# Four scheduling edits in a hybrid S5 and retention decoder layer: priority of the first evacuations and of the last chunk's scan, spacing of the chunks, issuing engine of sixteen copies

## The chip, the cores and the metric

The kernel runs on one core of a Trainium2 chip. The metric is the device time of one execution in microseconds (us); lower is better. The engines are named as in the profile: PE multiplies matrices, DVE works on vectors, ACT evaluates functions and copies, POOL does small vector work, SP issues transfers. A transfer can also be issued from ACT's instruction stream. Each engine takes its instructions in the order of its own queue.

## The reference, cut to what matters

One inference step of one decoder layer on 320 columns: 256 prompt positions, and 64 sample columns (8 sequences of 8 positions). All data are float32.

```python
proj = h @ w_in                                   # u, q, k, v, g
s5_out, s5_re, s5_im = s5_mixer(u, ...)           # diagonal state scan, 64 groups of 16 channels
o, ret_new = retention_chunked(q, k, v, ret0)     # 8 heads, decayed attention and state
o = (o - mu) * lax.rsqrt(var + NORM_EPS)          # per-head norm
ret_out = silu(g) * o * ret_gn_w
x = x + concat([s5_out, ret_out]) @ w_out
gate, up = split(rms_norm(x) @ w_ffn_in)
x = x + (silu(gate) * up) @ w_ffn_out
```

The S5 state follows `x[t] = lam_bar * x[t-1] + b_bar u[t]` and gives `y = Re(C x) + D u`, then a GELU and a gated unit. The retention states of the 8 sample sequences are updated too: `r_new = r * decay + k^T v`.

## The kernel before, in words

**Products.** Every weight block is split into two parts, `hi` (rounded) and `lo` (the rest), and a product is three PE passes: hi by hi, hi by lo, lo by hi. `wload` (line 121) loads half a weight block of 128 x 1024 values (`raw`), has ACT cast it to `hi` (line 130) and DVE subtract to get `lo` (line 131). Three buffers of `hi` and of `lo` are there, so a block's half can be prepared when an older half has been used up. `gemm` (line 135) issues the passes, 48 matmuls for 16 steps of k, into one of two PSUM accumulators (tag `acc`).

**Order of the work.** The orders of PE and POOL are written by hand. PE's is set by a model clock: a step of k (three matmuls) adds 0.4, and `run_due` after a step lets every waiting generator run whose due time has come, so its matmuls are put between two steps. The delays are in `DL` (line 807). The orders of DVE, ACT and SP are found by a list scheduler, which takes ready instructions by priority: the place in the program, moved ahead by the `offset` of `tc.high_priority`. `wload` has 3000, most evacuations of accumulators have `EVAC` = 1500.

**First stage** (lines 825 to 871). Four products run side by side into four accumulators: u of chunk 0 (`ps0`, the tile `py0`), u of chunk 1 (`ps1`, first half of `pb0`), q of head 0 (`pq`, second half of `pb0`), k of head 0 (`pk`, an `acc` accumulator). `finish_norm` (line 860) waits for the norm's factor `rbc`, multiplies the rotation tables `csr` by it with `EVAC` priority, and multiplies `ps0` and `ps1` into `u32` at lines 869 and 870 with none. At the same time DVE works through `s5_params` (line 363), a long chain of small operations on `tab` and `ecs`; from `ecs` POOL makes the tables of `s5_tables` (line 462), and only then, in POOL's written order, the norm of head 0 (`gy`, lines 704 to 711). ACT makes `on` from `gy` (line 714), PE transposes `on` into `pn` (line 725).

**Chunks.** `s5_chunk` (line 502) treats 8 groups of channels at a time, 8 chunks in all. It prepares its operators on DVE (`bl`, `cl`), has PE transpose them (`pt`), multiplies into `pb` (line 554), scans the states on DVE (lines 574 to 601: `t`, `ends`, `w`, the scan, `v`, then `xp`), and multiplies `xp` into `py` (lines 603 to 613). Chunk c starts when the model clock is at `T0 + PER * c`, `pt` comes 14.2 later, `pb` 6.6 after that, `py` 17.8 after that. After the last projection (`do_g(7)`), lines 912 and 913 run the model clock forward until the last chunk's `py` has been issued.

**After the projections.** `split_r` (line 945) splits the heads' outputs into `r4a` and `r4b` for the product with `w_out`; `r4a` lies in the memory of `tab`, which the last chunk's `v` still reads. `x1` is loaded from `xT` (line 907), into memory that the projections have read.

**Sample states.** During the first gate of the FFN `states_split` (line 1036), with an offset of 6000, splits `kv` into `kvh` and `kvl` in the weight buffers and spreads them with 16 copies from SBUF to SBUF (lines 1050 and 1051), 128 KB each, issued by SP. They write into `hi` and `lo` buffers that the first gate (`ps_fg`) has just read. `states_load` and `states_add` use them later.

Of the kernel before, what the change touches and what calls it, by code (L numbers as in the profile page):

```python
# [12 lines left out]
F32 = mybir.dt.float32  # L13
# [4 lines left out]
ADD, SUB, MUL = ALU.add, ALU.subtract, ALU.mult  # L18
PSUM = bass.MemoryType.PSUM

P = 128
# [12 lines left out]
NCP = NP // CH  # L34
NC = N // CH
# [9 lines left out]
def hybrid_kernel(ctx, tc, xT, w_in, w_in4, w_out, w_glu, w_fi, w_fo, vecs, s5p, bc, x0,  # L45
# [3 lines left out]
    pe, act, dve, pool, sp = nc.tensor, nc.scalar, nc.vector, nc.gpsimd, nc.sync  # L49
# [5 lines left out]
    def f(t):  # L55
        return t.bitcast(F32)
# [44 lines left out]
    def mm(cost, *a, **k):  # L101
        pe.matmul(*a, **k)
        clk.now += cost
# [71 lines left out]
    def tt(out, a, b, op):  # L175
        dve.tensor_tensor(out, a, b, op)  # L176
        return out
# [11 lines left out]
            stt(y, tmp, 1.5, y, ADD, MUL)  # L189

    STARTS = (0, 128, 192)

    def rstd_bcast(pool_, acc, ps_of, tag, last=None, dl=5.0, ytok=None):

        def sums(a, name):
            ps = ps_of(name)
            for i, s in enumerate(STARTS):
                mm(0.1, ps[:, i:i + 1], a[:, s:s + P], ones[:, 0:1], start=True, stop=True)
            return ps[:, 0:3]

        ms = pool_.tile([P, 3], F32, name="ms", tag=tag + "ms")
        y = pool_.tile([P, 3], F32, name="ry", tag=tag + "ry")
        if ytok is not None:
            ytok.append(y)
        tmp = pool_.tile([P, 3], F32, name="rt", tag=tag + "rt")
        ps = sums(acc, "ps_r")
        if last is not None:
            keep_warm(3)
        with tc.high_priority(offset=2000):
            ts(ms, ps, -0.5 / D, MUL, -0.5 * EPS, ADD)  # L210
            if last is not None:
                stt(ms, sums(last(), "ps_l"), -0.5 / D, ms, MUL, ADD)
            if last is not None:
                keep_warm(9)
            rsqrt(ms, y, tmp)
        yield dl
        ps2 = ps_of("ps_r2")
        for i, s in enumerate(STARTS):
            mm(0.22, ps2[:, s:s + P], y[:, i:i + 1].to_broadcast([P, P]), ident, start=True,
               stop=True)  # L220
        yield ps2[:, :N]
# [12 lines left out]
    s5 = s5stack.enter_context(tc.tile_pool(name="s5", bufs=1, side="right"))  # L234
# [9 lines left out]
    rbc = mp.tile([P, N], F32, name="rbc")  # L244
# [13 lines left out]
    u32 = up.tile([P, 8, N], F32, name="u32")  # L258
# [37 lines left out]
    x0t = s5.tile([P, 2, NPAIR, NB], F32, name="x0t")  # L296
    tab = s5.tile([P, 2, NPAIR, NCP], F32, name="tab", tag="tab", bufs=1)
# [10 lines left out]
    lx0 = s5.tile([P, 2, NPAIR, NB], F32, name="lx0")  # L308
    endp = s5.tile([P, 2, NPAIR], F32, name="endp")
    ends = s5.tile([P, 2, 2, NPAIR, NB], F32, name="ends")  # L310
# [186 lines left out]
    def load_bc(c):  # L497
        if c < 8:
            raws[c] = s5.tile([P, 2, 8, 16], F32, name="raw_bc", tag="raw_bc", bufs=3)
            sp.dma_start(raws[c], bc[:, c])  # L500

    def s5_chunk(c):
        load_bc(c + 2)
        js = slice(4 * c, 4 * c + 4)
        cl, xp, d0 = cls_[c % 2], xps[c % 2], d0s[c % 2]
# [19 lines left out]
        for w_, pc in ((0, gpc), (1, lpc)):  # L525
# [4 lines left out]
            if w_ == 0:  # L530

                bl = s5.tile([P, 2, 2, 2, CH, 16], F32, name="bl", tag="bl", bufs=1)
                for r, (a, b, op) in enumerate(((m1[:, 0:4], m2[:, 4:8], SUB), (m1[:, 4:8], m2[:, 0:4], ADD))):
                    a, b = (t_.rearrange("p (u q) e h -> p u q (e h)", q=2) for t_ in (a, b))
# [19 lines left out]
        pb = ps_b.tile([P, 2, 512], F32, name="pb", tag="pb", bufs=1)  # L554
        for i in range(4):
            for u in range(2):

                for g in range(2):
                    us, gs = slice(64 * u, 64 * u + 64), slice(64 * g, 64 * g + 64)
# [9 lines left out]
        for u in range(2):  # L569
            for g in range(2):  # L570
                hs = slice(16 * g, 16 * g + 16)
                act.copy(kbd[64 * g:64 * g + 64, 2 * u:2 * u + 2, hs],
                         pk_[64 * u:64 * u + 64, 0:64].rearrange("p (i h) -> p i h", h=32)[:, :, hs])
        pvs = [pb[:, u, 0:4 * NC].rearrange("p (r q t) -> p r q t", r=2, q=2) for u in range(2)]
        shr = [P, 2, 4, NCP]
        tb = [tab[:, q, js].unsqueeze(1).to_broadcast(shr) for q in range(2)]
        t = [s5.tile(shr, F32, name=f"t{q}", tag=f"m{q}", bufs=1) for q in range(2)]
        w = s5.tile(shr, F32, name="w", tag="w", bufs=1)
        for q in range(2):
            for u in range(2):  # L580
                us = slice(2 * u, 2 * u + 2)
                tt(t[q][:, :, us], pvs[u][:, :, :, 0:NCP], tb[q][:, :, us], MUL)
        for u in range(2):
            us = slice(4 * c + 2 * u, 4 * c + 2 * u + 2)
            psm = pvs[u][:, :, :, NCP:].rearrange("p r q (b s) -> p r q b s", s=2)
            tt(ends[:, 0, :, us], psm[:, :, :, :, 0], lx0[:, :, us], ADD)
            act.copy(ends[:, 1, :, us], psm[:, :, :, :, 1])
        tt(w[:, 0], t[0][:, 0], t[1][:, 1], ADD)
        tt(w[:, 1], t[0][:, 1], t[1][:, 0], SUB)
        wf = w.rearrange("p r j t -> p (r j t)")  # L590
        dve.tensor_tensor_scan(wf, d0.rearrange("p r j t -> p (r j t)"), wf, 0.0, MUL, ADD)
        act.copy(endp[:, :, js], w[:, :, :, NCP - 1])
        t = [s5.tile(shr, F32, name=f"v{q}", tag=f"m{q}", bufs=1) for q in range(2)]
        for q in range(2):
            tt(t[q], w, tb[q], MUL)
        tt(xp[:, 0, :, 1:NCP], t[0][:, 0, :, 0:NCP - 1], t[1][:, 1, :, 0:NCP - 1], SUB)
        tt(xp[:, 1, :, 1:NCP], t[0][:, 1, :, 0:NCP - 1], t[1][:, 0, :, 0:NCP - 1], ADD)
        xs = xp[:, :, :, NCP:].rearrange("p r j (b q) -> p r j b q", q=2)
        for r in range(2):
            act.copy(xs[:, r, :, :, 0], x0t[:, r, js])  # L600
            act.copy(xs[:, r, :, :, 1], ends[:, 0, r, js])
        yield DL["scan"]
        py = ps_y.tile([P, 512], F32, name="py", tag="y", bufs=1)
        for j in range(4):
            r = 32 * j
            mm(0.15, py[r:r + 32, 0:N], kbd[:, j], ush[:, j].rearrange("p s c -> p (s c)"), start=True,
               stop=False, tile_position=(0, r))
        for t in range(CH):
            for q in range(2):
                for j in range(4):  # L610
                    r = 32 * j
# [14 lines left out]

    EVAC = 1500
    GN = 1000  # L630
    GAM = [1.0 - 2.0 ** (-5.0 - h) for h in range(H)]
    rot_t = {}

    def rot(ps, name):
        assert rot_t["ready"]
        with tc.high_priority(offset=EVAC):
            return rot_(ps, name)
# [11 lines left out]
    def head_k(h, q_, qg, k_, R):  # L649
        yield DL["k"]  # L650
        pst = misc("pst")
        for i, s in enumerate(STARTS):
            tr(pst[:, P * i:P * i + P], k_[:, s:s + P])
# [9 lines left out]
        mk = R["mk"]  # L663
        with tc.high_priority(offset=EVAC):
            tt(sm[:, 0:256], pss[:, 0:256], mk[:, 0:NP], MUL)
# [5 lines left out]
    def head_v(h, v_, qg, rt, R):  # L671
        yield DL["v"] + (3.0 if h == 0 else 0.0)
        pst2 = misc("pst2")
        for i, s in enumerate(STARTS):
            tr(pst2[:, P * i:P * i + P], v_[:, s:s + P])
# [21 lines left out]
        y = mp.tile([P, 2, 4], F32, name="gy", tag="gy", bufs=1)  # L697
        with tc.high_priority(offset=GN):
            for i in range(4):
# [42 lines left out]
    def proj(i):  # L742
        return gemm("ps_p", w_in[i], KT, xhi, xlo)
# [7 lines left out]
    def do_u(c):  # L751
        ps = proj(c)
        with tc.high_priority(offset=EVAC):
            tt(u32[:, c], ps, rbc, MUL)
# [24 lines left out]
    def do_v(h, ps=None):  # L779
        ps = proj(10 + 4 * h) if ps is None else ps  # L780
        R = HS[h]
        v_ = mp.tile([P, N], F32, name="v_", tag="v_", bufs=1)
        with tc.high_priority(offset=EVAC):
            act.copy(v_, ps)
# [3 lines left out]
    def sg_mul(h, sg):  # L788
        while "gn" not in HS[h]:
            yield 1.0  # L790
        if "sg" in HS[h]:
            return
        with tc.high_priority(offset=EVAC):
            tt(retp[:, h], retp[:, h], sg, MUL)
        HS[h]["sg"] = True

    def do_g(h):
        ps = proj(11 + 4 * h)
        sg = mp.tile([P, N], F32, name="sg", tag="sg", bufs=2)
        with tc.high_priority(offset=EVAC):  # L800
            tt(sg, ps, rbc, MUL)
# [4 lines left out]

    DL = dict(b1=14.2, b2=6.6, scan=17.8, k=8.5, v=6.1,
              o=2.2, u=6.0, c=10.0, n2=2.4, n2b=2.6, nm=0.8)
    T0, PER = 54.6, 34.0


    clk.now = 8.0
# [12 lines left out]
    for k1 in (1, *range(2, KT + 1, 2)):  # L825
        with tc.high_priority(offset=100000), tc.manual_schedule(engines={mybir.EngineType.SP}):
# [3 lines left out]
            q = slice(k0 % 2, (k1 - 1) % 2 + 1)  # L830
# [19 lines left out]
    ps0, ps1, pq, pk = accs  # L850
# [9 lines left out]
    def finish_norm():  # L860
        next(rg)
        act.copy(rtok, ytok[0])
        yield 4.5
        rps = next(rg)
        with tc.high_priority(offset=EVAC):
            act.copy(rbc, rps)
            tt(csr[:, 0], csr[:, 0], rbc, MUL)
            tt(csr[:, 1], csr[:, 1], rbc, MUL)
        tt(u32[:, 0], ps0, rbc, MUL)
        tt(u32[:, 1], ps1, rbc, MUL)  # L870
        rot_t["ready"] = True

    spawn(finish_norm(), DL["nm"])
# [30 lines left out]
    xp = ctx.enter_context(tc.tile_pool(name="xp", bufs=1, reuse_waits="tile"))  # L904
# [96 lines left out]
    for n in range(KT):  # L1001
# [8 lines left out]
        else:  # L1010
            s = square(n, hp)
# [22 lines left out]
    SU = {}  # L1034

    def states_split():

        with tc.high_priority(offset=6000):
            states_split_()

    def states_split_():
        kvh, kvl = (wp.tile([P, 8, P], F32R, name=n, tag=n, bufs=3) for n in ("hi", "lo"))
        act.copy(kvh, kv)
        tt(kvl, kv, f(kvh), SUB)
        SU["k"] = [wp.tile([P, 8, P], F32R, name="hi", tag="hi", bufs=3) for _ in range(2)]
        SU["v"] = [wp.tile([P, 8, P], F32R, name="lo", tag="lo", bufs=3) for _ in range(2)]
        for i in range(2):
            for a in range(4):
                d = slice(32 * a, 32 * a + 32)
                sp.dma_start(f(SU["k"][i][d]), f((kvh, kvl)[a // 2][64 + 32 * i:96 + 32 * i]))  # L1050
                sp.dma_start(f(SU["v"][i][d]), f((kvh, kvl)[a % 2][32 * i:32 * i + 32]))

    def states_load(h):
        rt = wp.tile([P, NB, P], F32, name="raw", tag="raw", bufs=3)
# [181 lines left out]
```

## Time and profile before

| | |
|---|---|
| median of 3 runs (lowest to highest) | 1475.02 us (1472.91 to 1475.27) |
| the profiled execution | 1475.36 us, of it 1473.6 us span |
| busy in the span: PE, DVE, ACT, POOL | 98%, 58%, 41%, 7% |
| granted PE clock, mean | 0.993 |

The profile records every instruction of one execution. Times are counted from the first instruction. Idle time before an instruction stands in brackets with the engine that ended it. A PE that is busy by the profile need not run at full clock; the granted clock is listed for each stretch. The span is divided among the projections and the mixers (to 368 us), the output product and the gated unit (to 520 us), the FFN, and a tail.

### The profile page before, as it was taken

To read this page: it belongs to the slowest core of one execution; us is meant where nothing else is said; L and a number is where in the kernel's file an instruction comes from. 1 tells how busy PE (TensorE), PEld (TensorE's weight loads), DVE (VectorE), ACT (ScalarE), POOL (GpSimd) and SP (SyncE) were. 2 spreads that over 40 slices of the span, in tenths; PEclk is the share of its full clock that TensorE was granted. 3 is DMA by queue.
4 is the path that set the end of the run, shared out by engine and by line. 5 is a ranking of instruction groups with operands and counts; after the bars stand their busy time and mean duration, and the time that the engine had idled before them with its cause. 6 is when DMAs were issued, how large, how long until landed. Compare 5 with 4: busy or idle time off the path is not lost.

```text
span 1473.6 us, 26372 instructions
## 1 busy us (share of the span) xinstructions
PE 1444.0 (98%) x10654; PEld 1426.7 (97%) x10654; DVE 854.3 (58%) x1405; ACT 607.6 (41%) x973; POOL 101.8 (7%) x228
## 2 busy tenths in 40 slices
PE   8999999999899999999999999999999999999997
PEld 8899999999899999999999999999999999999996
DVE  8887776777656765565444444444444445444454
ACT  6455555554335543333333333333333333333352
POOL 1324404210000000000000000000000000000001
PEclk9999999999999999999999999999999999999999
DMA  8555554544544474665444455444445544445443
GB/s 260 167 152 159 159 164 155 156 151 133 188 148 147 154 243 162 223 212 175 148 153 146 123 154 171 151 154 147 134 144 153 171 150 151 146 123 156 151 145 111
DMA packets 84713, 235.39 MB, mean 160 GB/s; under 512 B 16368, under 2 KB 32368, under 8 KB 84592
## 3 DMA queue, kind: packets, MB, share of 16 engines
q1 hardware_dynamic: 84448, 233.68, 49.8%
q8 instruction: 84, 1.38, 0.4%
q14 instruction: 37, 0.30, 0.1%
q10 hardware_dynamic: 144, 0.04, 0.0%
HBM read 222.63 MB, written 8.95 MB: 157 GB/s over the span
## 4 chain that ended last, share of the span: by engine, by line
PE 69%; DVE 1%; issue 0%; ACT 0%; DVEq 0%
PE ps_fo L143 7%; PE ps_fo L142 7%; PE ps_fu L143 7%; PE ps_fu L142 7%; PE ps_fu L141 7%; PE ps_fo L141 7%; PE ps_fg L143 7%; PE ps_fg L141 7%; PE ps_fg L142 7%; PE ps_o L142 1%; PE ps_o L141 1%; PE ps_o L143 1%; PE ps_g L142 1%; PE ps_g L143 1%; PE ps_g L141 1%; DVE x L176 0%
## 5 line engine op out<-in xcount | busy, mean ns | idle before, releaser
L131 DVE TENSOR_TENSOR lo<-raw,hi 128x1024 fp32r<-128x1024 f32 (+1 forms) x416 | 468.1, 1126 | 392.1 <-ACT hi L130 391.2
L130 ACT CAST hi<-raw 128x1024 fp32r<-128x1024 f32 (+1 forms) x416 | 402.0, 967 | 680.1 <-PE ps_fo L142 189.3
L141 PE MATMUL ps_fg<-hhi,hi 128*128 128x320 f32 x704 | 217.7, 309 | 1.1 <-ACT hi L130 1.1
L143 PE MATMUL ps_fg<-hhi,lo 128*128 128x320 f32 x704 | 217.6, 309 | 0.7 <-DVE lo L131 0.7
L141 PE MATMUL ps_fo<-ahi,hi 128*128 128x320 f32 x704 | 217.6, 309 | 0.0
L142 PE MATMUL ps_fo<-alo,hi 128*128 128x320 f32 x704 | 217.6, 309 | 0.0
L143 PE MATMUL ps_fo<-ahi,lo 128*128 128x320 f32 x704 | 217.6, 309 | 0.0
L142 PE MATMUL ps_fu<-hlo,hi 128*128 128x320 f32 x704 | 217.5, 309 | 0.0
L142 PE MATMUL ps_fg<-hlo,hi 128*128 128x320 f32 x704 | 217.5, 309 | 0.0
L141 PE MATMUL ps_fu<-hhi,hi 128*128 128x320 f32 x704 | 217.4, 309 | 0.0
L143 PE MATMUL ps_fu<-hhi,lo 128*128 128x320 f32 x704 | 217.4, 309 | 0.0
L141 PE MATMUL ps_p<-xhi,hi 128*128 128x320 f32 x560 | 178.4, 318 | 5.2 <-DVE sg L176 3.2
L143 PE MATMUL ps_p<-xhi,lo 128*128 128x320 f32 x560 | 173.9, 311 | 0.7 <-DVE lo L131 0.7
L142 PE MATMUL ps_p<-xlo,hi 128*128 128x320 f32 x560 | 173.6, 310 | 0.0
L141 PEld LDWEIGHTS ps_fg<-hhi,hi 128*128 128x128 f32 x704 | 132.4, 188 | 1.6 <-ACT hi L130 1.3
L143 PEld LDWEIGHTS ps_fg<-hhi,lo 128*128 128x128 f32 x704 | 132.4, 188 | 1.0 <-DVE lo L131 1.0
L142 PEld LDWEIGHTS ps_fg<-hlo,hi 128*128 128x128 f32 x704 | 132.4, 188 | 0.3
L142 PEld LDWEIGHTS ps_fu<-hlo,hi 128*128 128x128 f32 x704 | 132.4, 188 | 0.0
L141 PEld LDWEIGHTS ps_fu<-hhi,hi 128*128 128x128 f32 x704 | 132.4, 188 | 0.0
L143 PEld LDWEIGHTS ps_fu<-hhi,lo 128*128 128x128 f32 x704 | 132.4, 188 | 0.0
L141 PEld LDWEIGHTS ps_fo<-ahi,hi 128*128 128x128 f32 x704 | 132.2, 188 | 0.0
L142 PEld LDWEIGHTS ps_fo<-alo,hi 128*128 128x128 f32 x704 | 132.2, 188 | 0.0
(402 smaller groups left out, 1977.9 us busy)
## 6 DMA issues: line engine op xcount, KB each, us to landing
raw<-w_fi SPq DMA_DIRECT2D x176, 512.0 KB, 3.7
raw<-w_in SPq DMA_DIRECT2D x79, 512.0 KB, 4.0
raw<-w_fo SPq DMA_DIRECT2D x64, 512.0 KB, 3.5
raw<-w_out SPq DMA_DIRECT2D x32, 512.0 KB, 3.7
raw<-w_fo SPq DMA_DIRECT2D x64, 192.0 KB, 2.4
rt<-r SPq DMA_DIRECT2D x8, 512.0 KB, 5.0
raw<-w_glu SPq DMA_DIRECT2D x8, 512.0 KB, 3.6
raw<-r SPq DMA_DIRECT2D x8, 512.0 KB, 4.0
```

What stands on the lines that cost most here:

```text
L130: act.copy(hi[:, :m], raw[:, :m])
L131: dve.tensor_tensor(lo[:, :m], raw[:, :m], f(hi[:, :m]), SUB)
L141: pe.matmul(ps, hi, xhi[:, k], start=k == 0, stop=False)
L142: pe.matmul(ps, hi, xlo[:, k], start=False, stop=False)
L143: pe.matmul(ps, lo, xhi[:, k], start=False, stop=k == nk - 1)
```

## The change

Lines 574 to 601 become a function `s5_scan`, word for word, called with a priority offset for chunk 7 alone (0 for the others). `EVAC` and `GN` are only defined earlier. The two evacuations in `finish_norm` move into the block with `EVAC` priority. `T0` and `PER` become smaller. `states_split` loses its priority, and its 16 copies are issued by ACT.

```diff
+    EVAC = 1500
+    GN = 1000
...
+    def s5_scan(c, pb, xp, d0):
+        js = slice(4 * c, 4 * c + 4)
         pvs = [pb[:, u, 0:4 * NC].rearrange("p (r q t) -> p r q t", r=2, q=2) for u in range(2)]
...
+        with tc.high_priority(offset=2 * EVAC if c == 7 else 0):
+            s5_scan(c, pb, xp, d0)
         yield DL["scan"]
...
-    T0, PER = 54.6, 34.0
+    T0, PER = 53.6, 33.4
...
-        tt(u32[:, 0], ps0, rbc, MUL)
-        tt(u32[:, 1], ps1, rbc, MUL)
+            tt(u32[:, 0], ps0, rbc, MUL)
+            tt(u32[:, 1], ps1, rbc, MUL)
...
     def states_split():
-
-        with tc.high_priority(offset=6000):
-            states_split_()
-
-    def states_split_():
         kvh, kvl = (wp.tile([P, 8, P], F32R, name=n, tag=n, bufs=3) for n in ("hi", "lo"))
...
-                sp.dma_start(f(SU["k"][i][d]), f((kvh, kvl)[a // 2][64 + 32 * i:96 + 32 * i]))
-                sp.dma_start(f(SU["v"][i][d]), f((kvh, kvl)[a % 2][32 * i:32 * i + 32]))
+                act.dma_start(f(SU["k"][i][d]), f((kvh, kvl)[a // 2][64 + 32 * i:96 + 32 * i]))
+                act.dma_start(f(SU["v"][i][d]), f((kvh, kvl)[a % 2][32 * i:32 * i + 32]))
```

## Rows read from the trace of the kernel before

**Rows 1.** The page: busy time; the costliest groups (busy us, mean ns).

```profile
PE 1444.0 (98%) x10654; PEld 1426.7 (97%) x10654; DVE 854.3 (58%) x1405; ACT 607.6 (41%) x973; POOL 101.8 (7%) x228
...
L131 DVE TENSOR_TENSOR lo<-raw,hi 128x1024 fp32r<-128x1024 f32 (+1 forms) x416 | 468.1, 1126 | 392.1 <-ACT hi L130 391.2
```

**Rows 2.** PE's waits in the whole span: us in total, times, longest us.

```profile
PE py L102 <- DVE xp L176: 6.2, 1, 6.2
PE ps_p L141 <- DVE sg L176: 3.2, 1, 3.2
...
PE ps_p L141 <- DVE k__3502 L176: 1.3, 1, 1.3
...
PE ps_fg L141 <- ACT hi L130: 1.1, 1, 1.1
PE ps_fg L143 <- DVE lo L131: 0.7, 1, 0.7
```

**Rows 3.** PE's timeline, last chunk (first row: chunk 6): start, us, instruction.

```profile
344.43 1.29 PE L102 MATMUL py<-xp,cl 128*32 128x80 f32 x64
...
368.27 0.74 PE L102 MATMUL py<-ush,kbd 128*32 128x320 f32 x8
375.25 2.43 PE L102 MATMUL py<-xp,cl 128*32 128x80 f32 x64 [6.23 <-DVE xp L176]
...
380.94 0.31 PE L159 MATMUL ps_o<-r4a,hi 128*128 128x320 f32 x1
```

**Rows 4.** Stretches: us, busy PE (x), PEld, DVE, ACT, POOL, granted clock, DMA.

```profile
58.00:60.00 2.00, 2.00 (x9) 2.00 (x8) 2.00 (x11) 0.00 (x0) 0.47 (x1) 0.50 0.93 290
...
376.00:378.00 2.00, 2.00 (x53) 1.78 (x45) 1.21 (x6) 0.00 (x0) 0.00 (x0) 0.50 1.00 384
...
1000.00:1100.00 100.00, 100.00 (x684) 100.00 (x684) 47.62 (x61) 34.69 (x44) 0.00 (x0) 1.00 0.45 142
```

**Rows 5.** DVE's timeline, last chunk, from its first to its last product.

```profile
359.90 0.76 DVE L176 TENSOR_TENSOR t<-pb,tab 128x256 f32<-128x256 f32 x2 [1.60 <-PE pb L102]
...
373.48 1.29 DVE L176 TENSOR_TENSOR r4b<-retp,r4b 128x320 fp32r<-128x320 f32 x3
374.69 0.74 DVE L176 TENSOR_TENSOR xp<-v,v 128x252 f32<-128x252 f32 x2
```

**Rows 6.** The tile x: from 365 to 390 us, landing of its four loads.

```profile
DMA to landing us min/median/max: 5.9/7.4/10.1
```

**Rows 7.** PE's and ACT's timelines at the first evacuations.

```profile
56.71 0.60 PE L141 MATMUL ps_p<-xhi,hi 128*128 128x320 f32 x1 [3.23 <-DVE sg L176]
...
53.26 0.42 ACT L641 COPY sw<-pb 64x320 f32<-64x320 f32 x1 [2.31 <-DVE u L176]
```

**Rows 8.** Timelines of POOL, ACT and PE: from the tables to the head's norm.

```profile
59.53 0.57 POOL L474 COPY tab<-ecs 128x8 f32<-128x8 f32 x1 [51.73 <-DVE ecs L176]
...
73.65 0.24 POOL L704 TENSOR_SCALAR mv<-mv 128x4 f32<-128x4 f32 x1
...
78.21 1.50 ACT L714 ACTIVATE on<-po,gy 128x128 f32<-128x128 f32 x4 [3.92 <-POOL gy L711]
...
78.86 1.24 PE L107 MATMUL pn<-ident,on 128*128 128x128 f32 x4
```

**Rows 9.** Timelines of SP, ACT and PE at the copies of the sample states.

```profile
525.22 0.60 SPq L1050 DMA_DIRECT2D hi<-hi  x1
...
535.38 48.67 SPq L129 DMA_DIRECT2D raw<-w_fi  x18
...
525.31 1.05 ACT L130 CAST hi<-raw 128x1024 fp32r<-128x1024 f32 x1 [2.81 <-DMA raw<-w_fi]
...
529.65 0.31 PE L141 MATMUL ps_fu<-hhi,hi 128*128 128x320 f32 x1
```

**Rows 10.** DMA issues: queue, count, KB each, median us to landing.

```profile
hi<-hi SPq DMA_DIRECT2D x4, 128.0 KB, 2.9
```

**Rows 11.** The tile kst: issues on SP, ns min/median/max, first and last start.

```profile
L515 SPq DMA_DIRECT2D kst<-via x64: 325/424/1349, 56.8 to 336.3; - x64
```

More of the change, by code (lines that the diff above doesn't have):

```diff
@@ L500, in load_bc @@
             sp.dma_start(raws[c], bc[:, c])
+    def s5_scan(c, pb, xp, d0):
+        js = slice(4 * c, 4 * c + 4)
+        pvs = [pb[:, u, 0:4 * NC].rearrange("p (r q t) -> p r q t", r=2, q=2) for u in range(2)]
+        shr = [P, 2, 4, NCP]
+        tb = [tab[:, q, js].unsqueeze(1).to_broadcast(shr) for q in range(2)]
+        t = [s5.tile(shr, F32, name=f"t{q}", tag=f"m{q}", bufs=1) for q in range(2)]
+        w = s5.tile(shr, F32, name="w", tag="w", bufs=1)
+        for q in range(2):
+            for u in range(2):
+                us = slice(2 * u, 2 * u + 2)
+                tt(t[q][:, :, us], pvs[u][:, :, :, 0:NCP], tb[q][:, :, us], MUL)
+        for u in range(2):
+            us = slice(4 * c + 2 * u, 4 * c + 2 * u + 2)
+            psm = pvs[u][:, :, :, NCP:].rearrange("p r q (b s) -> p r q b s", s=2)
+            tt(ends[:, 0, :, us], psm[:, :, :, :, 0], lx0[:, :, us], ADD)
+            act.copy(ends[:, 1, :, us], psm[:, :, :, :, 1])
+        tt(w[:, 0], t[0][:, 0], t[1][:, 1], ADD)
+        tt(w[:, 1], t[0][:, 1], t[1][:, 0], SUB)
+        wf = w.rearrange("p r j t -> p (r j t)")
+        dve.tensor_tensor_scan(wf, d0.rearrange("p r j t -> p (r j t)"), wf, 0.0, MUL, ADD)
+        act.copy(endp[:, :, js], w[:, :, :, NCP - 1])
+        t = [s5.tile(shr, F32, name=f"v{q}", tag=f"m{q}", bufs=1) for q in range(2)]
+        for q in range(2):
+            tt(t[q], w, tb[q], MUL)
+        tt(xp[:, 0, :, 1:NCP], t[0][:, 0, :, 0:NCP - 1], t[1][:, 1, :, 0:NCP - 1], SUB)
+        tt(xp[:, 1, :, 1:NCP], t[0][:, 1, :, 0:NCP - 1], t[1][:, 0, :, 0:NCP - 1], ADD)
+        xs = xp[:, :, :, NCP:].rearrange("p r j (b q) -> p r j b q", q=2)
+        for r in range(2):
+            act.copy(xs[:, r, :, :, 0], x0t[:, r, js])
+            act.copy(xs[:, r, :, :, 1], ends[:, 0, r, js])
     def s5_chunk(c):
@@ L573, in s5_chunk @@
                          pk_[64 * u:64 * u + 64, 0:64].rearrange("p (i h) -> p i h", h=32)[:, :, hs])
[L574 to L601, printed above, removed]
+        with tc.high_priority(offset=2 * EVAC if c == 7 else 0):
+            s5_scan(c, pb, xp, d0)
         yield DL["scan"]
@@ L624, in s5_chunk @@
             s5_state["done"] = True
-    EVAC = 1500
-    GN = 1000
     GAM = [1.0 - 2.0 ** (-5.0 - h) for h in range(H)]
```

## The prediction

> **What bounds the kernel now.** The page comes first: PE is busy 98% of the span [rows 1], and the change takes no matmul away. It can only win PE's idle time and the time that PE runs at half clock. The list of PE's waits says who ends that idle time [rows 2]; five of its entries lie near the edits: 6.2 us for `xp` of the last chunk, 3.2 us for an evacuation (`sg`) after the norm, 1.3 us for `k` of head 4, and 1.1 and 0.7 us for `hi` and `lo` of an FFN weight. Together 12.5 us, 0.8% of the time. The stretches then show what a long wait costs behind it: the granted clock is 0.50, the 1.2 GHz level, from 58 to 60 us and from 376 to 378 us, after the two longest of these waits, and 1.00 in the steady FFN, where a matmul takes 100 us / 684 = 0.146 us [rows 4]. The timelines around each wait, last, tell whether its time is free to be won.
>
> **The last chunk: 8.9 us.** PE's first part of `py` starts at 368.27, then PE waits 6.23 us for `xp` [rows 3]. From 375.25 to 380.94 it does the second part and twelve `w_out` matmuls: 5.69 us, where chunk 6's second part took 1.29 us [rows 3] and twelve matmuls at full clock take 12 x 0.146 = 1.75 us. So 2.65 us went to the half clock, and the stall costs 6.23 + 2.65 = 8.9 us.
>
> Two edits act on it, and either nearly suffices. The start of chunk 7 moves by 1.0 + 7 x 0.6 = 5.2 of the model clock; a step of 0.4 there is three matmuls, 0.44 us, so `pb` comes 5.2 / 0.4 x 0.44 = 5.7 us earlier, while `py` stays behind the last projection, which it already followed at once. DVE's chain ran from 359.90 to 375.43 [rows 5]; begun 5.7 us earlier it ends at 369.7, against 375.25 - 6.23 = 369.0, when PE asks. The priority then takes out of the chain what doesn't belong to it: the three `r4b` splits right ahead of `xp` alone are 1.29 us [rows 5]. I take the wait as gone, and the clock with it. The price is that the chain may hold up a weight's `lo` on DVE; each is 1.13 us [rows 1] and is prepared half a gemm, 24 x 0.146 = 3.5 us, or more before its use, so I cost it at 0, at most one `lo`, 1.1 us.
>
> What is late next? `r4b` of the last head was split at 374.8 [rows 5]; PE would ask for it after `py` (369.0 + 1.29), 24 matmuls of `r4a` and nine of `r4b` (4.8 us), at 375.1. Without the chain in the way DVE and ACT have it sooner. The loads of `x1` are issued from 368.4 and take 5.9 to 10.1 us [rows 6]: the first lands between 374.3 and 378.5, and the third output block needs its accumulator free after 48 matmuls, at 377.3. Between 0 and 1.2 us; I take 0, as the first issued is nearest to the shortest landing.
>
> **The first evacuations: 0.** The wait before 56.71 is for `sg`, behind the two multiplications into `u32` on DVE and, through them, ACT's copies `sw` (idle 2.31 us until `u`) [rows 7]. With priority the two go right after the tables `csr`, and q, `sg` and k follow sooner: 3.2 us of wait, and with some 1.5 us of half clock (between 0 and the 2.65 of the last chunk) 4.7 us. But that is the whole at 57 us. At 78.86 PE transposes `on` of head 0, and it came there only 0.3 us after ACT's first of four pieces (1.50 / 4 each): ACT had idled 3.92 us for POOL, POOL reached that norm at 73.65 after tables begun at 59.53, and these had waited for `ecs` [rows 8]. The change moves the two multiplications within the DVE work that already lay ahead of that `ecs`; it takes nothing out. So `on` comes no sooner, PE stands at `pn` 4.7 us early, and the gain is given back there. Bounds: +4.7 us if `on` also comes sooner, and a loss of two `lo`, 2.3 us, if a faster PE pulls DVE's prioritised work ahead of `ecs`. I take 0, the value of the chain as it stands.
>
> **The spacing of the other chunks: 0.** Chunk c comes 1.1 to 5.1 us sooner, and DVE's bursts meet other heads. Before, one of them cost a wait, 1.3 us for `k` [rows 2]. It may go, stay, or have a twin: +1.3 to -1.3 us.
>
> **The sample states' copies: 1.8 us.** SP issues 16 copies from 525.22; the next weight load of the FFN leaves at 535.38 [rows 9], and its `hi` and `lo` are the waits of 1.1 and 0.7 us. Each copy takes 10.16 / 16 = 0.635 us of SP. On ACT they leave SP free, so the loads go out some ten us earlier and this wait goes: 1.8 us. The 10.2 us now stand in ACT's queue, behind them its casts, one per 3.5 us at 1.05 us each; spread out they fit, and the lost offset lets casts (3000) go first. What costs is a block. The first eight can start when the gate's first half is read, at about 525.2; at 525.31 ACT casts the up product's first weight, which PE uses at 529.65 [rows 9]. Eight copies ahead of it (5.1 us) move its `lo` to 525.3 + 5.1 + 1.05 + 1.13 = 532.6, a stall of 2.9 us. Bounds: +1.8 to -2.9 us and, as after 3.2 us, up to 1.5 us of clock. I take +1.8, as the cast carries the higher priority.
>
> The row of a copy's landing, 2.9 us against 0.635 us of issue [rows 10, 9], bears on a rule. The Trainium skill, "DMA: Bandwidth & Descriptors", section "Issuing engines are not separate DMA queues", says that issuing from several engines saves only the sequencer's time, usually small beside the transfer. By it this part would give about 0. The row speaks against "small" here: the issue times of sixteen add up in front of a load.
>
> **Sum.** The profiled execution took 1475.36 us (span 1473.6 and 1.8 around it), 0.34 above the median. 1475.36 - 8.9 - 0 - 0 - 1.8 = 1464.7; against the median of 1475.02 that is **1464.3 us**.
>
> **Rivals.**
> - *The first evacuations' gain is kept.* For: 4.7 us are really lost there. Against: rows 8. 1464.3 - 4.7 = 1459.6 us.
> - *ACT's copies come in a block of eight ahead of the cast.* For: at 525.2 both become ready within 0.1 us. Against: priority. 1464.3 + 1.8 + 2.9 = 1469.0 us, with the clock 1470.5.
> - *Moving the issue saves nothing*, because the loads are then held by the transfers. For: 16 x 128 KB of copies still move at the same time. Against: the load left only after the last copy [rows 9]. 1464.3 + 1.8 = 1466.1 us. The Trainium skill's rule above would make this of it.
> - *The last chunk does not profit*, its wait taken over by another of equal length (`r4b`, `x1`). For: `r4b` was ready 0.3 us before the time at which it is then wanted. Against: its delay came from the chain itself. 1475.0 - 1.8 = 1473.2 us, within 0.2%.
> - *Slower:* all sixteen copies stand on ACT ahead of the first cast. At p us each the stall is 525.3 + 16p + 2.2 - 529.65 = 16p - 2.15, plus 2.65 of half clock. It outweighs the 8.9 + 1.8 from p = 0.64 on, just SP's own pace, and at the longest issue that a small copy took, 1.35 us [rows 11], it is 22.1 us: 1486.4 us. Against: the second eight wait for the gate's second half, and casts go first.
>
> **How the numbers follow.** My forecast 0.56, evacuations kept 0.13, block of eight 0.15, issue saves nothing 0.07, last chunk without profit 0.05, slower 0.04. The range of 1459.5 to 1470.0 takes in the first four but for the block with its clock, and the bounds of chunks and `lo`. A measurement of this kernel can tell about 0.2%, 3 us. Faster by more: 0.91; within: 0.05; slower: 0.04.
>
> **What would show it.** Right: no wait of PE for `xp`, full clock from 366 to 385 us, no wait in the second FFN gate, and a new wait of 3 to 5 us at `pn` near 75 to 79 us while the one before 56.7 is short. Wrong: `pn` without a wait and everything after it 4 us sooner; PE waiting for `hi` of the first `ps_fu` with copies ahead of it on ACT; or a wait for `r4b` or an accumulator after `py`.

## The result and the profile after

The kernel after takes 1464.2 us (median of 4 runs, 1463.93 to 1465.08), the one before 1474.97 us (median of 4, 1472.91 to 1475.27). The ratio is 0.9931, with a 95% interval from 0.9914 to 0.9948: 10.8 us less. The profiled execution of after took 1463.95 us, 1461.8 us of it span, against 1475.36 and 1473.6 us. The forecast was 1464.3 us.

The page answers to [rows 1]. PE has the same 10654 matmuls, and it is busy for 4.2 us less (1439.8 against 1444.0): the same matmuls took less time. Of this, 3.4 us lie ahead of the FFN, where fewer matmuls ran at half clock. The queue line q10 had 144 packets before; the copies' 768 packets moved there from q1.

```profile
PE 1439.8 (98%) x10654; PEld 1423.1 (97%) x10654; DVE 853.1 (58%) x1405; ACT 607.6 (42%) x973; POOL 101.7 (7%) x228
...
q10 hardware_dynamic: 912, 2.14, 0.5%
```

PE's waits of after, as in [rows 2] (us in total, times, longest):

```profile
PE pn L107 <- ACT on L720: 2.3, 1, 2.3
...
PE ps_p L141 <- DVE k__3551 L176: 1.1, 1, 1.1
...
PE ps_p L141 <- DVE k__794 L176: 0.5, 1, 0.5
```

Gone are `xp` (6.2), `sg` (3.2), the two of `ps_fg` (1.1 and 0.7) and `k__3502` (1.3). New are `on` at `pn` (2.3), `k__3551` (1.1) and `k__794` (0.5). All five waits that the prediction named (12.5 us) are gone, and 3.9 us came back in other places.

**The last chunk.** PE's timeline, as in [rows 3] (start, us, instruction):

```profile
367.49 0.75 PE L102 MATMUL py<-ush,kbd 128*32 128x320 f32 x8
368.06 1.29 PE L102 MATMUL py<-xp,cl 128*32 128x80 f32 x64
...
371.14 0.31 PE L159 MATMUL ps_o<-r4a,hi 128*128 128x320 f32 x1
```

The second part of `py` follows the first without a bracket, so without a wait, and takes 1.29 us as in a chunk at full clock. The last row shown is the matmul that stood at 380.94 before: 9.80 us earlier. At `py` the lead was 368.27 - 367.49 = 0.78 us, so the last chunk itself gave 9.0 us. The stretches, as in [rows 4] (us, busy PE, PEld, DVE, ACT, POOL, granted clock, DMA), have the clock at 1.00, its 2.4 GHz level, at 58 us as well:

```profile
58.00:60.00 2.00, 1.73 (x13) 1.68 (x13) 1.94 (x13) 1.36 (x5) 1.02 (x6) 1.00 0.75 249
...
368.00:370.00 2.00, 2.00 (x73) 1.82 (x66) 1.70 (x4) 2.00 (x5) 0.00 (x0) 1.00 0.86 257
...
376.00:378.00 2.00, 2.00 (x15) 2.00 (x15) 2.00 (x4) 1.05 (x1) 0.00 (x0) 1.00 1.00 415
```

DVE's timeline, as in [rows 5], shows the chain begin at 354.04, 5.9 us earlier than before, and end at 361.0, 7 us before PE asks. `r4b` now comes behind it and still in time:

```profile
354.04 1.41 DVE L176 TENSOR_TENSOR t<-pb,tab 128x256 f32<-128x256 f32 x4
...
360.25 0.75 DVE L176 TENSOR_TENSOR xp<-v,v 128x252 f32<-128x252 f32 x2
...
370.52 1.29 DVE L176 TENSOR_TENSOR r4b<-retp,r4b 128x320 fp32r<-128x320 f32 x3
```

**The first evacuations.** Timelines of PE, POOL, ACT and PE again, as in [rows 7, 8]:

```profile
54.00 0.41 PE L141 MATMUL ps_p<-xhi,hi 128*128 128x320 f32 x1 [0.53 <-DVE k__794 L176]
...
58.32 0.55 PE L107 MATMUL pst<-ident,v__798 128*128 128x128 f32 x3 [0.27 <-ACT kv L663]
...
58.82 0.20 POOL L477 COPY tab<-ecs 128x8 f32<-128x8 f32 x1 [51.01 <-DVE ecs L176]
...
73.40 0.24 POOL L710 TENSOR_SCALAR mv<-mv 128x4 f32<-128x4 f32 x1
...
76.65 1.51 ACT L720 ACTIVATE on<-po,gy 128x128 f32<-128x128 f32 x4 [8.12 <-POOL gy L717]
...
77.16 1.38 PE L107 MATMUL pn<-ident,on 128*128 128x128 f32 x4 [2.31 <-ACT on L720]
```

In before the second of these rows is

```profile
62.51 0.55 PE L107 MATMUL pst<-ident,v__798 128*128 128x128 f32 x3 [0.27 <-ACT kv L657]
```

so PE leads by 2.7 us at the third projection (54.00 against 56.71) and by 4.2 us at head 0's `v`, where the half clock no longer stands in between; 1.2 us of both leads are the earlier start of `csr` (47.37 against 48.55, below). At `pn` it waits for 2.31 us and keeps a lead of 1.7 (77.16 against 78.86). POOL still works through the tables from 58.82 before it reaches head 0's norm at 73.40, 0.25 us earlier than before.

**The copies.** Timelines of SP, ACT's queue, ACT and PE, as in [rows 9]:

```profile
510.04 11.00 SPq L129 DMA_DIRECT2D raw<-w_fi  x7
...
515.45 0.61 ACTq L1051 DMA_DIRECT2D hi<-hi  x1
...
533.70 1.05 ACT L130 CAST hi<-raw 128x1024 fp32r<-128x1024 f32 x1 [2.47 <-DMA hi<-lo]
533.72 0.52 ACTq L1052 DMA_DIRECT2D lo<-lo  x1
...
551.27 0.51 ACTq L1052 DMA_DIRECT2D lo<-lo  x1
```

SP issues weight loads only. The 16 copies lie between ACT's casts from 515.45 to 551.27, one or two to a cast.

**A ruler for all runs.** Between executions the first stage starts at different times, because one early transfer comes sooner or later (last section). So each profile is cut at three marks: DVE's first product into `csr`, the first weight load of the FFN's gate (`ps_fg`), and that of its output product (`ps_fo`). The rows of before, then of after:

```profile
48.55 0.88 DVE L176 TENSOR_TENSOR csr<-csr,rbc 128x320 f32<-128x320 f32 x2
...
L141 PEld LDWEIGHTS ps_fg<-hhi,hi x704: 186/188/192, 520.4 to 1295.4; 128*128 128x128 f32 x176
...
L141 PEld LDWEIGHTS ps_fo<-ahi,hi x704: 187/188/189, 838.2 to 1457.3; 128*128 128x128 f32 x176
```

```profile
47.37 0.89 DVE L176 TENSOR_TENSOR csr<-csr,rbc 128x320 f32<-128x320 f32 x2
...
L141 PEld LDWEIGHTS ps_fg<-hhi,hi x704: 187/188/192, 510.6 to 1282.9; 128*128 128x128 f32 x176
...
L141 PEld LDWEIGHTS ps_fo<-ahi,hi x704: 187/188/189, 825.8 to 1444.9; 128*128 128x128 f32 x176
```

For before that is 520.4 - 48.55 = 471.9, 838.2 - 520.4 = 317.8, and 1473.6 - 838.2 = 635.4 us. The same three rows give the table for all kernels (us; the first four numbers add up to the span):

| kernel | `csr` at | to `ps_fg` | to `ps_fo` | to the end | median |
|---|---|---|---|---|---|
| before | 48.55 | 471.9 | 317.8 | 635.4 | 1474.97 |
| after | 47.37 | 463.2 | 315.2 | 636.0 | 1464.20 |
| e1_evac | 47.32 | 471.9 | 318.1 | 635.4 | 1474.43 |
| e2_scan | 47.83 | 465.0 | 318.0 | 635.3 | 1467.27 |
| e3_space | 47.61 | 462.8 | 319.5 | 635.4 | 1464.90 |
| e4_copies | 46.98 | 471.2 | 315.2 | 636.0 | 1470.67 |
| e5_no_scan_prio | 46.91 | 463.3 | 315.1 | 636.0 | 1463.46 |
| e6_tables_late | 47.64 | 460.4 | 315.2 | 636.0 | 1460.83 |
| e7_act_prio | 46.27 | 463.3 | 328.1 | 636.3 | 1476.40 |
| e8_sp_no_prio | 47.70 | 463.3 | 320.0 | 635.4 | 1468.20 |
| e9_tables_only | 47.68 | 460.6 | 315.2 | 636.0 | 1460.79 |
| e10_no_evac | 47.03 | 462.9 | 315.1 | 636.1 | 1463.23 |
| e11_after_again | 46.51 | 463.3 | 315.1 | 636.1 | 1463.74 |
| e12_tables_again | 46.19 | 460.4 | 315.1 | 636.0 | 1459.19 |

For two profiles of one kernel the ruler repeats to 0.1 us (after, e11; e6, e12), where medians of the same kernel differ by up to 1.6 us. It is not always that fine: before and e4, whose code is the same up to `ps_fg`, differ by 0.7 us there, and e2 and e3, whose code is the same from there on, by 1.5 us in the next column, where e3 alone fell to half clock. For after against before it says: 1.2 us by chance of the start, 8.7 us between `csr` and the FFN, 2.6 us in the FFN's first part, and 0.6 us lost at the end. With the rounding that is 11.8 us, the difference of the spans. A further 0.3 us is lost outside the span: the executed time is 2.1 us longer than the span in after and 1.8 us in before.

### The profile page after: what moved, and what is told of

Read it like the earlier page. It is cut to its first block, busy times and chain, and to the rows that moved or that the text cites. A ratio compares the mean times of both kernels' runs of the same rounds, so it can differ in the third digit from the quotient of the medians.

```text
span 1461.8 us, 26364 instructions
## 1 busy us (share of the span) xinstructions
PE 1439.8 (98%) x10654; PEld 1423.1 (97%) x10654; DVE 853.1 (58%) x1405; ACT 607.6 (42%) x973; POOL 101.7 (7%) x228
## 4 chain that ended last, share of the span: by engine, by line
PE 70%; DVE 0%; issue 0%; ACT 0%; DVEq 0%
PE ps_fg L141 7%; PE ps_fo L143 7%; PE ps_fo L142 7%; PE ps_fu L143 7%; PE ps_fg L143 7%; PE ps_fu L142 7%; PE ps_fg L142 7%; PE ps_fu L141 7%; PE ps_fo L141 7%; PE ps_o L143 1%; PE ps_o L141 1%; PE ps_o L142 1%; PE ps_g L142 1%; PE ps_g L143 1%; PE ps_g L141 1%; DVE x L176 0%
```

## The experiments

They were run in three groups, each beside its own runs of before (medians 1474.38, 1474.02 and 1474.49 us). The first four kernels are before with one of the four edits.

**e1_evac: before, with the two multiplications into `u32` under `EVAC` priority.**

```diff
-        tt(u32[:, 0], ps0, rbc, MUL)
-        tt(u32[:, 1], ps1, rbc, MUL)
+            tt(u32[:, 0], ps0, rbc, MUL)
+            tt(u32[:, 1], ps1, rbc, MUL)
```

> The kernel before with one edit: the two multiplications into u32 get EVAC priority. My theory (the gain is given back at pn, because POOL makes the tables ahead of head 0's norm): PE's wait before the third projection falls from 3.2 to about 0.5 us and its half clock goes, PE then waits 2 to 3 us for on at pn, and what is left at 85 us is 1.5 us, the amount by which on comes sooner in the changed kernel; 1473.5 us. Rival, the gain is kept: no wait at pn, 1470.3 us. Rival, it is lost wholly or turns into a loss: 1475 us or more.

Measured: 1474.43 us, ratio 1.0004 [0.9995, 1.0013]. The wait for `sg` is gone, and its time stands at `pn`:

```profile
PE pn L107 <- ACT on L714: 2.3, 1, 2.3
```

The ruler gives 471.9 us, that of before to the tenth. The edit alone is worth nothing, where I had expected 1.5 us; the rival that expected 1470.3 us falls.

**e2_scan: before, with `s5_scan` and its priority for chunk 7.**

```diff
+        with tc.high_priority(offset=2 * EVAC if c == 7 else 0):
+            s5_scan(c, pb, xp, d0)
```

> The kernel before with one edit: the last chunk's scan gets priority 3000, the spacing stays. My theory (either edit alone nearly suffices): the chain still starts at 359.9 and now takes some 7 us, as in the changed kernel, so xp is there by 367, ahead of the 369 at which PE asks; no wait, no half clock, 8.9 us less: 1466.1 us. Rival, the earlier start is what counts: xp after 370, a wait of 1 us or more stays, 1467 to 1471 us.

Measured: 1467.27 us, ratio 0.9953 [0.9941, 0.9966]. The wait for `xp` is gone, but another stands behind it. DVE's and PE's timelines of e2:

```profile
366.70 0.74 DVE L176 TENSOR_TENSOR xp<-v,v 128x252 f32<-128x252 f32 x2
...
370.90 0.88 DVE L176 TENSOR_TENSOR r4a<-retp,r4a 128x320 fp32r<-128x320 f32 x2
...
371.84 0.41 PE L160 MATMUL ps_o<-r4a,hi 128*128 128x320 f32 x1 [1.64 <-DVE r4a L176]
```

The priority shortens the chain from 15.5 us to 8.3 (359.19 to 367.4), but `r4a` follows it, in the memory of `tab` that the chain's `v` reads, and PE asks for it right after `py`. The ruler gives 465.0 us: 6.9 of the 8.7 us. By the medians it is 7.1 us less than before, where 8.9 were expected.

**e3_space: before, with the chunks closer together.**

```diff
-    T0, PER = 54.6, 34.0
+    T0, PER = 53.6, 33.4
```

> The kernel before with one edit: T0 and PER as in the changed kernel. My theory: the last chain begins 5.7 us sooner and still takes some 15 us, so xp comes at about 369.7, a wait of about 0.7 us without half clock; 8.2 us less, minus up to 0.8 us that the closer chunks cost between 85 and 367 us: 1466.8 to 1467.6 us. Rival, the priority is what counts: a wait of 3 us or more stays, 1470 us or more.

Measured: 1464.9 us, ratio 0.9939 [0.9927, 0.9952]: better than either number expected. DVE's and PE's timelines of e3, without any priority on the scan:

```profile
353.81 1.08 DVE L176 TENSOR_TENSOR t<-pb,tab 128x256 f32<-128x256 f32 x3
...
361.47 0.41 DVE L176 TENSOR_TENSOR xp<-v,v 128x252 f32<-128x252 f32 x1
...
367.85 1.29 PE L102 MATMUL py<-xp,cl 128*32 128x80 f32 x64
```

Begun 6.1 us earlier, the chain takes 8.1 us instead of 15.5 by itself: DVE's rows between its first `t` and `xp` hold one `lo` in e3, in before three and all splits of `r4a` and `r4b`, which in e3 come behind `xp`. The ruler gives 462.8 us, all of the gain. Its FFN, where SP still issues the copies, has the old waits of 1.2 and 0.7 us, and this time half clock behind them (stretches of e3; 319.5 us on the ruler):

```profile
534.00:536.00 2.00, 2.00 (x9) 2.00 (x8) 1.25 (x2) 0.21 (x1) 0.00 (x0) 0.50 0.74 248
```

**e4_copies: before, with the copies on ACT and without the offset.**

```diff
-        with tc.high_priority(offset=6000):
-            states_split_()
...
-                sp.dma_start(...)
+                act.dma_start(...)
```

> The kernel before with one edit: states_split without priority, its copies issued by ACT. My theory: the waits of 1.1 and 0.7 us in the second FFN gate go, nothing comes in their place, 1.8 to 2.0 us less: 1473.0 us. Rival (only the issue time moves, the loads are held by the transfers): the waits stay, 1475.0 us. Rival (copies stand ahead of casts on ACT): a wait of 2.9 us at the first up product, 1476 us or more.

Measured: 1470.67 us, ratio 0.9976 [0.9967, 0.9985]. Both waits of `ps_fg` are gone, and that stretch is 317.8 - 315.2 = 2.6 us shorter. The end is 0.6 us longer, as in every kernel whose copies ACT issues, and 0.3 us more is lost outside the span (2.1 against 1.8 us in all eleven runs): 1.7 us net. The medians differ by more, 3.7 us (2.2 to 4.9 by the interval), where 1.8 to 2.0 us were expected. In e4's profile 0.7 us more are won ahead of the FFN, where it runs the same code as before; what the medians show beyond the 1.7 us is not explained by the edit.

**e5_no_scan_prio: after, without the scan's priority.**

```diff
-        with tc.high_priority(offset=2 * EVAC if c == 7 else 0):
+        with tc.high_priority(offset=0):
```

> The changed kernel without the priority of the last chunk's scan. My theory (the earlier start alone nearly suffices): the chain takes some 15 us again, xp comes within 1 us of the time at which PE asks; 0 to 1 us more than the changed kernel: 1464.2 to 1465.2 us. Rival, the priority carries the gain: a wait of 3 us or more and half clock behind it, 1468 us or more.

Measured: 1463.46 us, ratio 0.9924 [0.9912, 0.9937], 463.3 us on the ruler against 463.2, and no wait that after doesn't have. On top of the spacing the priority adds nothing. The chain takes 8.1 us (353.53 to 361.60), as in e3 and not the 15 us that I expected again.

**e6_tables_late: after, with group 0's tables on POOL behind head 0's norm.**

```diff
-                for _ in s5_tables(ec, es, g):
-                    pass
+                rot_t["tab0"] = s5_tables(ec, es, g)
...
         pool.tensor_tensor(w_, m_, y_, MUL)
+        if h == 0:
+            for _ in rot_t["tab0"]:
+                pass
```

> The changed kernel with POOL's tables for the first two chunks written behind head 0's norm instead of ahead of it. My theory (POOL's order holds on, and on holds PE): the norm comes right after the statistics at about 66 us, the wait of 2.3 us at pn goes and with it most of the 0.7 and 0.5 us behind it; the tables end near 85 us, ahead of the first chunk's scan at 95; 2 to 3 us less than the changed kernel: 1461.2 to 1462.2 us. Rival, on waits for DVE's statistics or ACT's queue anyway: less than 0.5 us. Rival, the tables now come late for the first chunk's scan: slower than 1464.2 us.

Measured: 1460.83 us (1458.22 to 1461.37), ratio 0.9905 [0.9891, 0.9919]; repeated as e12 below. It beats both kernels, and the wait at `pn` is gone, as the theory of POOL's order has it.

**e7_act_prio: after, with the old offset of 6000 around the copies on ACT.**

```diff
+        with tc.high_priority(offset=6000):
+            states_split_()
```

> The changed kernel with the offset of 6000 back on states_split, copies on ACT. My theory (a block of copies ahead of casts is what ACT's queue can't take): eight or more copies at 0.6 us each stand ahead of the first up product's casts, PE waits 3 us or more there; 1467 to 1475 us. Rival, the issues on ACT cost nothing wherever they stand: 1464.2 us.

Measured: 1476.4 us (11 runs), ratio 1.0014 [1.0005, 1.0024]: slower than before. Timelines of ACT's queue and ACT in e7, then PE's waits:

```profile
514.38 0.61 ACTq L1056 DMA_DIRECT2D hi<-hi  x1
...
525.12 0.60 ACTq L1057 DMA_DIRECT2D lo<-lo  x1
525.76 2.94 ACT L130 CAST hi<-raw 128x1024 fp32r<-128x1024 f32 x3 [14.13 <-DMA hi<-hi]
```

```profile
PE ps_fu L141 <- ACT hi L130: 8.2, 1, 8.2
...
PE ps_fu L143 <- DVE lo L131: 1.8, 1, 1.8
```

All sixteen stand ahead of the first cast, for 11.3 us. PE waits 10.0 us for `hi` and `lo`, and on the ruler the stretch is 328.1 - 315.2 = 12.9 us longer, so 2.9 us went to the half clock.

**e8_sp_no_prio: after, with the copies on SP, still without the offset.**

```diff
-                act.dma_start(...)
+                sp.dma_start(...)
```

> The changed kernel with the copies back on SP, without the priority. My theory (it is the block ahead of the loads that costs, not the engine): the scheduler puts the copies between the loads, no wait of 1 us in the second FFN gate; within 0.5 us of the changed kernel: 1464.2 to 1464.7 us. Rival, the engine is what counts: the waits of 1.1 and 0.7 us are back, 1466 us.

Measured: 1468.2 us, ratio 0.9958 [0.9946, 0.997], 4.0 us slower than after: my expectation was wrong. Timelines of SP, DVE and PE in e8:

```profile
564.91 0.33 SPq L129 DMA_DIRECT2D raw<-w_fi  x1
565.29 1.38 SPq L1052 DMA_DIRECT2D lo<-lo  x1
...
571.86 0.69 DVE L176 TENSOR_TENSOR hi<-lo,bmk 128x512 fp32r<-128x512 f32 x1
...
572.64 0.47 PE L1070 MATMUL psu<-hi 128*128 128x512 f32 x1 [2.73 <-issue]
```

SP puts one or two copies behind each load, and the loads come 3.5 us apart; the last copy leaves at 565.3, where ACT had sent it at 551.3. The first state update begins at 569.5, its second matmul waits 2.73 us, and half clock follows (320.0 against 315.2 us on the ruler). So freeing the loads was one half of the edit, and having the copies done by `psu` is the other. The profile names "issue" there; the cause is read from the rows. The second matmul needs DVE's second product of the spread copies with the mask `bmk`, which ends at 572.55, 0.09 us before it; in after that product begins at 557.00, 11.8 us ahead of its matmuls. The last copy left at 565.3, and copies of its line took up to 6.7 us to land.

**e9 to e12: the evacuations and the tables, two by two, on one chip.** e11 is after, e10 after without the evacuations' priority, e12 is e6 again, e9 is e6 without the evacuations' priority.

> The kernel after with two edits: the chirp tables of group 0 stand on POOL behind head 0's norm (as in e6_tables_late), and the two evacuations into u32 lose their priority again. Theory (POOL's tables in front of head 0's norm are the gate, and the first evacuations are worth something only once that gate is gone): the wait for sg near 57 us is back, 2 to 3 us, with some half clock behind it; the norm comes early, so PE keeps no slack at pn to give it back, and the kernel is 2 to 4 us above e12_tables_again: 1463 to 1465 us. Rival A (the first evacuations are worth nothing wherever the gate stands): equal to e12_tables_again within 1 us, about 1461. Rival B (the gain of the late tables came from the evacuations alone): as before's first stage, 1464 and a wait at pn.

> The kernel after with only the two evacuations into u32 without priority. Theory (their gain is given back at pn): a wait for sg near 57 us, none or under 1 us for on at pn, and the time of e11_after_again within 0.7 us, about 1464.2. Rival (they give what the wait lost, 3 to 5 us): 1467 to 1469 us.

> The kernel after, once more, as the companion of the other three on this chip: 1464.2 us, with a wait for on at pn of 1 to 3 us and none for sg.

> The kernel of e6_tables_late once more (first evacuations with priority and tables behind the norm). Theory: 1460.8 us, 3 to 4 us under e11_after_again. Rival (the difference was the earlier landing of a load in that execution): within 1 us of e11_after_again.

Measured: e9 1460.79 us, ratio 0.9905 [0.989, 0.9921]; e10 1463.23 us, 0.9924 [0.9911, 0.9936]; e11 1463.74 us, 0.9929 [0.9916, 0.9941]; e12 1459.19 us, 0.9897 [0.9884, 0.9911].

| ruler to `ps_fg` | evacuations without priority | with |
|---|---|---|
| tables first (as before) | e10 462.9 | after, e11 463.2, 463.3 |
| tables behind the norm | e9 460.6 | e6, e12 460.4, 460.4 |

The tables' place is worth 2.3 to 2.9 us. The evacuations' priority is worth -0.3 to -0.4 us with the tables first and 0.2 us with them late, all less than the 0.7 us by which the ruler can be off. I had expected 2 to 4 us of it in e9, and that was wrong: rival A holds by the ruler. The medians of e9 and e12, 1.6 us apart, could not tell it alone; of the 1.8 us between the two profiled executions 1.5 stand at the start (47.68 against 46.19), and e6, the same kernel as e12, has e9's median. Timelines of POOL, ACT and PE in e12 show where it goes:

```profile
64.40 0.63 POOL L709 TENSOR_SCALAR mv<-mv 128x4 f32<-128x4 f32 x1 [56.69 <-DVE tab L176]
...
68.64 1.51 ACT L722 ACTIVATE on<-po,gy 128x128 f32<-128x128 f32 x4 [2.51 <-POOL gy L716]
...
73.70 0.60 PE L107 MATMUL pn<-ident,on 128*128 128x128 f32 x4
...
84.47 0.42 PE L143 MATMUL ps_p<-xhi,lo 128*128 128x320 f32 x1 [1.52 <-DVE lo L131]
...
89.23 0.41 PE L141 MATMUL ps_p<-xhi,hi 128*128 128x320 f32 x1 [0.82 <-DVE k__1174 L176]
```

The norm is now early (`on` at 68.64, no wait at `pn`), and PE, ahead of its helpers once more, waits ten microseconds later, for DVE. The stretches from 80 to 90 us of e9, then of e12:

```profile
80.00:90.00 10.00, 10.00 (x71) 9.99 (x71) 9.97 (x16) 4.47 (x6) 9.53 (x13) 1.00 0.50 153
```

```profile
80.00:90.00 10.00, 7.66 (x52) 7.13 (x51) 9.92 (x15) 3.97 (x7) 9.47 (x17) 1.00 0.34 102
```

DVE is busy for 9.9 of 10 us in both. In e9 PE lost its time at `sg` (1.9 us, and half clock behind it) and then runs through; in e12 it keeps that time and gives it back here.

## Why the prediction was right, point by point

**The last chunk: 8.9 us forecast, 9.0 measured.** Wait and half clock are both gone, as worked out. One step of the working was wrong in size: I moved DVE's chain by 5.7 us and kept its 15.5 us, so that it ended at 369.7; begun earlier it takes 8.1 us by itself (e3, e5) and ends at 361.9. "Either nearly suffices" was right in kind, but not even-handed: spacing alone gives all of it (e3), the priority alone leaves 1.8 us (e2), and on top of the spacing it gives nothing (e5). Another step that failed is in "what is late next": I named `r4b` and `x1` and wrote that without the chain in the way DVE has the splits sooner. With priority alone the chain goes in front of `r4a`'s splits, and PE waited 1.64 us for those. In the kernel after the spacing keeps it from showing. Nothing is waited for there behind `py`.

**The first evacuations: 0 forecast, 0 measured** (e1: 0.0 us on the ruler against before, 0.7 the wrong way against e4; after against e10: 0.3 us the wrong way). The lost 4.7 us that I worked out were in part those of one execution. PE asked for the third projection at 53.5 us in before and in e10, both without the evacuations' priority. In before, `csr` came at 48.55, the latest of all fourteen profiles, and PE waited 3.23 us with half clock behind it; in e10 it came at 47.03, and the wait was shorter, at full clock to head 0's `v` (clock 1.00 from 54 to 62 us):

```profile
55.20 0.39 PE L141 MATMUL ps_p<-xhi,hi 128*128 128x320 f32 x1 [1.74 <-DVE sg L176]
```

So the lead at `v` was real, but counted from `csr` it is 3.0 us against before and 1.6 us against e10, and that is why the wait at `pn` (2.3) is shorter than the 3 to 5 us that I gave as its sign. Of the 1.7 us that PE kept there 1.2 are the earlier start, which is chance. "It takes nothing out" was right, and a little of the loss that I had only as a bound came true: POOL's tables begin 11.44 to 11.53 us behind `csr` in the six kernels with that priority and the tables first, 10.98 to 11.00 in the five without it. Against that POOL's rows from the tables to the end of the norm took 17.8 us instead of 18.4 to 18.7, so `on` came at nearly the same distance from `csr`. What I had wrong was the picture of a single gate: e9 and e12 show that behind POOL stands DVE, full from 80 to 90 us.

**The spacing of the other chunks: 0 forecast, 0 alone.** At the last `py` e3 leads before by 368.27 - 367.28 = 0.99 us, of which 48.55 - 47.61 = 0.94 is the start; e10, with the spacing and without the evacuations' priority, by 1.53 with 1.52 of start. In after the lead is 0.78 with 1.18 of start, so both edits together lose 0.4 us, inside the bounds. The wait for `k__3502` (1.3) went and got its twin, `k__3551` (1.1).

**The copies: 1.8 us forecast, 2.6 in their stretch, 1.7 with the longer end and the 0.3 us outside the span.** The two waits were sized right; some 0.8 us more stands in no wait that the profile lists: PE is busy that much longer for the same matmuls (315.86 against 315.07 us in that stretch), though the granted clock is 1.00 in both. I had left it out, and the losses at the end I had not foreseen either. That the sum of the three lies near 1.8 is luck. ACT's casts were not held up, because the scheduler spread the copies among them.

**The rivals.** *Evacuations kept* falls by e1 and e10. *Block of eight* did not happen; its price was right in kind: *slower*, the block of sixteen, is e7. My formula, with the 11.3 / 16 = 0.71 us per copy that e7 shows, gives 16 x 0.71 - 2.15 + 2.65 = 11.9 us; the medians of e7 and after differ by 12.2, and with 0.71 above the break-even of 0.64 e7 is indeed slower than before. (*Block of eight* added back the 1.8 us that the freed loads win and this formula did not; e7 has no wait of `ps_fg`, so the formula had it right.) What decided between 1464 and 1476 us is the offset that the change drops. *Moving the issue saves nothing* falls by e4. The Trainium skill, "DMA: Bandwidth & Descriptors", section "Issuing engines are not separate DMA queues", says that issuing from several engines saves only the sequencer's time, usually small beside the transfer. The first half agrees with the traces: the same bytes moved, and no copy landed faster from ACT (medians of 3.5 to 4.1 us against 2.7 to 3.0). "Small" does not: the issues took 10.2 us of SP's queue in front of a load, and that stretch became 2.6 us shorter without them. *The last chunk without profit* was not borne out.

**The sum** came out within 0.1 us of the median, which is better than its parts and so in part luck: +0.1 (last chunk), -0.4 (chunks with evacuations), +0.8, -0.6 and -0.3 us (copies) nearly cancel, and the start of the first stage moves by more than any of these from one execution to the next.

**Left open:** spacing and copies together, without the two priorities, were not run; by the ruler they should equal after, while the medians of e3 and e4 alone add up to 13.2 us, 2.4 more than after wins, which their intervals allow. Why the end is 0.6 us longer with copies on ACT was not tried. The rows place it behind the last issue of an output transfer, which ends 4.0 us before the span does in before and 4.6 us in after.

## What to carry to other kernels

An engine that is let go earlier may run into the next thing that is late, so follow it to the next place where it needs each helper, and ask which helper is full there: here POOL's tables at 59 us, then DVE at 80 to 90 us, took back what the evacuations gave, and the gain came from moving POOL's work, not DVE's. Before giving a chain priority, see whether it can simply begin earlier: the earlier start halved the chain's length without pushing anything in front of PE. And a transfer's issue is work in a queue: sixteen small copies cost 2.6 us in front of weight loads, 12 us in one block ahead of casts, and 4 us when they stood behind the loads and came late; what has to be set is both what they stand in front of and by when they must be done.

## What the runs showed of the hardware that was not expected

**One early transfer moved whole profiles.** ACT waits for the second `raw_bc` and then makes `cl`; `csr` follows 5.16 to 5.18 us after that row in all fourteen profiles, whatever the edits. ACT's timeline of before, then of e12:

```profile
43.39 1.05 ACT L521 ACTIVATE cl<-raw_bc 64x64 f32<-64x64 f32 x4 [3.04 <-DMA raw_bc<-bc]
```

```profile
41.02 1.06 ACT L555 ACTIVATE cl<-raw_bc 64x64 f32<-64x64 f32 x4 [1.64 <-DMA raw_bc<-bc]
```

The row moves between 41.02 and 43.39, and the start of the first stage with it (46.19 to 48.55). Both parts of the transfer vary: SP issues it between 36.75 and 38.15 us, and the row begins 4.1 to 6.5 us after the issue. In e6 and e12, the same kernel, the row lies 1.4 us apart, which is nearly all of the 1.5 us between their spans. Over all profiles it is 2.4 us, as much as the copies' edit is worth.

**A copy's issue ran beside ACT's computing.** In after the copy at 533.72 begins 0.02 us after the start of the 1.05 us cast in front of it and is issued before that cast ends. Spread among casts, with one cast per 3.5 us, the sixteen issues of 0.51 to 0.61 us left no wait of PE in that stretch; in a row ahead of the casts, in e7, they held the casts for 11.3 us, and PE waited for 10.0.
